# Another DMA queue for one K tile, a key that the rope writes twice, and later transposes in a two-layer trunk on one core

## The chip, the cores and the metric

One Trainium2 chip, one core. The metric is the device time of one execution in microseconds. The kernel before takes 310.66 us, the median of three runs (310.49 to 310.70). All intermediate times are microseconds from the start of the profiled span, unless marked otherwise.

## The reference

Two layers of a post-norm trunk on x of 256 tokens by 1024 features (float32): `x = layer_norm(ALPHA * x + sublayer(x))`. The first is an attention in which an indexer selects 64 keys for each query, the second a stick-breaking attention. The change lies in the first:

```python
q, k, v, g, qi, wi, ki = split(x @ w_in)          # 16 heads of 64, indexer: 8 heads of 64, one key
q = apply_rope(q); k = apply_rope(k)
qi = apply_rope(qi); ki = apply_rope(ki)
rel = relu(einsum('bqhd,bsd->bqhs', qi, ki) * 64 ** -0.5)
score = einsum('bqhs,bqh->bqs', rel, wi * 8 ** -0.5)
score = where(key_chunk <= q_chunk, score, -inf)
_, idx = top_k(score, 64)
p = softmax(logits of q with the selected k)
return (p @ selected v * silu(g)) @ w_out
```

The second layer computes `z = q @ k`, a reversed running sum of `log_sigmoid(-z)` over earlier keys, and weights v with `exp(log_sigmoid(z) + sum)`, with the same gate, projection and norm.

## The kernel before, in words

Products of float32 values are made of three products of a shorter type (fp32r): every operand is split into a high part and a remainder. `split` (lines 65 to 68) does it for weights: ACT casts the high part `wh` (L66), DVE subtracts to get the remainder `wl` (L67). `feat_split` (L250 to L256) does the same for what comes out of a transpose, and `pad_split` (L258) splits a key for two heads in two halves of 64 partitions each, so it issues two ACT casts and two DVE remainders (L252, L253).

**Start.** x, transposed, and the indexer's weights arrive as eight K tiles of `x_idx` (L168 to L176), 420 KB each. Tile 0 comes in three pieces, two on SP's DMA queue and one on ACT's; tiles 1 and 3 are issued from ACT, the others from SP. PE multiplies them tile by tile (L231). Then weights come in chunks of 512 KB from `w_all`, all on SP's queue in program order (`load`, L79). There are four raw buffers, so the load of a chunk waits until DVE has made the remainder of the chunk four before it. I call the chunks w0, w1 and so on.

**Indexer.** `rope` (L214 to L221) makes two products (L218 with the cosine, L219 with the sine) and one sum (L221) on DVE. For each of two token tiles it is called for five heads and for four, the last of which is the indexer's key. POOL copies the key once more behind itself (L241), so that one transpose of two heads gives the key in both halves of the partitions. `select` transposes the doubled key (L275), splits it, transposes the eight query heads in two groups of four (L281), splits them (`qih`, `qil`), and then makes scores: three matmuls for each pair of heads and token tile (`mm3`, L141 to L143), a relu on ACT (`rel`, L294) and two score updates on DVE (L297). The selection of the 64 largest follows on DVE (L304, L305).

**Blocks of q, k and v.** `tok_block` (L121) multiplies four chunks into two of the three PSUM banks of pool `pp` (L118). `q_block` ropes its two banks, transposes them in eight transposes (L329) and splits them (L255, L256), all at its end. `k_block` ropes only, and `keys0` transposes a pair of heads later (L404). `v_block` copies its banks on ACT (L357). Line 527 mixes q, k and v of the first half with `select`; line 528 lists what fills in behind: k, q and v of the second half, the gates (L150, L152), the output projection (L118 with `oh`, `ol`).

**Attention.** The loop at L535 runs a pipeline over head pairs: keys, logits (L141 to L143), a softmax (DVE L423, ACT L428 and L433), transposes of it (PE L442 to L444, ACT copy L446), value matmuls (L372, L373).

The text above gives an order of program; a scheduler then fixes the order of instructions on each engine, and each engine runs its own in that order and waits where an operand is not there.

Of the kernel before, what the change touches and what calls it, by code (L numbers as in the profile page):

```python
# [14 lines left out]
P = 128  # L15
# [27 lines left out]
def trunk(ctx: ExitStack, tc: tile.TileContext, x_rows, x_idx, w_all, consts, lnp, out):  # L43
# [60 lines left out]
    def bank(p, w=512):  # L104
        return p.tile([P, 512], F32, name="bank", tag="bank")[:, :w]
# [6 lines left out]
    def tok_part(outs, src, wc, c):  # L112

        for xp, wp in ((0, 0), (1, 0), (0, 1)):
            for t, ps in outs:
                for k in range(2):
                    kk = 2 * c + k
                    nc.tensor.matmul(ps, src[kk][xp][:, t * P:(t + 1) * P], wc[wp][:, k, :],  # L118
                                     start=kk == 0 and xp + wp == 0, stop=kk == 7 and wp == 1)

    def tok_block(src):  # L121

        ps = [bank(pp) for _ in range(NT)]
        for c, wc in enumerate(load_block()):
            if c:
                yield
            tok_part(list(enumerate(ps)), src, wc, c)
        return ps

    def mix(*gens):  # L130
# [37 lines left out]
    for k in range(KT):  # L168
        raw = wraw.tile([P, CW], F32, name="raw", tag="raw")[:, :S + IDX_W]
        if k:  # L170
            (nc.scalar.dma_start if k in (1, 3) else load)(raw, x_idx[k])
        else:
            first = S + IDX_A
            load(raw[:, :S], x_idx[k, :, :S])
            nc.scalar.dma_start(raw[:, S:first], x_idx[k, :, S:first])
            load(raw[:, first:], x_idx[k, :, first:])  # L176
        wh = wspl.tile([P, CW], F32R, name="wh", tag="wh")[:, :IDX_W]
        wl = wspl.tile([P, CW], F32R, name="wl", tag="wl")[:, :IDX_W]
        if k:
            split(xTh[:, k], xTl[:, k], raw[:, :S])  # L180
        else:
            nc.vector.tensor_copy(xTh[:, k], raw[:, :S])
            nc.vector.tensor_sub(xTl[:, k], raw[:, :S], as32(xTh[:, k]))
        for c in cuts if k == 0 else (slice(0, IDX_W),):
            copy = split(wh[:, c], wl[:, c], raw[:, S + c.start:S + c.stop])
            if k == 0:
                tc.keep_in_program_order(copy)
        idx_w.append((wh, wl))
# [22 lines left out]
        nc.gpsimd.memset(as32(zl), 0.0)  # L211
        zpad.append((zh, zl))

    def rope(dst, ps, heads, t):  # L214
        v = ps.rearrange("p (h d) -> p h d", d=HD)
        a = wk.tile([P, 8, HD], F32, name="ra", tag="ra")[:, :heads]
        b = wk.tile([P, 8, HD], F32, name="rb", tag="rb")[:, :heads]
        nc.vector.tensor_mul(a, v, cos[:, t, None, :].to_broadcast([P, heads, HD]))  # L218
        nc.vector.tensor_mul(b, v, sin[:, t, None, :].to_broadcast([P, heads, HD]))  # L219
        halves = [u.rearrange("p h (e d) -> p h e d", e=2) for u in (dst, a, b)]  # L220
        nc.vector.tensor_add(halves[0], halves[1], halves[2][:, :, ::-1, :])  # L221


    psi = [[bank(at) for _ in range(2)] for t in range(NT)]
# [12 lines left out]
    for t in range(NT):  # L237
        r = sb.tile([P, D], F32, name=f"ri{t}", tag=f"x{t}")[:, :10 * HD].rearrange("p (h d) -> p h d", d=HD)
        rope(r[:, :5], psi[t][0][:, :IDX_A], 5, t)
        rope(r[:, 5:9], psi[t][1][:, :4 * HD], 4, t)  # L240
        nc.gpsimd.tensor_copy(r[:, 9], r[:, 8])  # L241
        w = few.tile([P, IH], F32, name=f"wi{t}")
        nc.vector.tensor_scalar(w, psi[t][1][:, 4 * HD:4 * HD + IH], float(np.float32(IH ** -0.5)), None,
                                op0=OP.mult)
        ri.append(r)
        wi.append(w)
# [22 lines left out]
    def select():  # L269

        for _ in range(2):
            yield
        pt = bank(at)
        for t in range(NT):
            nc.tensor.transpose(pt[:, t * P:(t + 1) * P], ri[t][:, 8:10, :], ident)  # L275
        pad_split(kz, pt[:, :S])
        for j in range(2):
            pt = bank(at)
            for a in range(2):
                for t in range(NT):  # L280
                    nc.tensor.transpose(pt[:, (2 * a + t) * P:(2 * a + t + 1) * P],  # L281
                                        ri[t][:, 4 * j + 2 * a:4 * j + 2 * a + 2, :], ident)
            pv = pt.rearrange("p (a s) -> p a s", a=2)
            feat_split(qih[:, 2 * j:2 * j + 2], qil[:, 2 * j:2 * j + 2], pv)
        yield
        scores = [sb.tile([P, (t + 1) * P], F32, name=f"sc{t}") for t in range(NT)]
        for j in range(4):
            for t in range(NT):
                n = (t + 1) * P
                ts = slice(t * P, (t + 1) * P)  # L290
                pv = bank(at, 2 * n).rearrange("p (a s) -> p a s", a=2)
                mm3(pv, qih[:, j, ts], qil[:, j, ts], kz[0][:, :, :n], kz[1][:, :, :n], True, True)
                rel = wk.tile([P, 2, S], F32, name="rel", tag="p256")[:, :, :n]
                nc.scalar.activation(rel, pv, AF.Relu, scale=SCALE)  # L294
                for a in range(2):
                    h = 2 * j + a
                    nc.vector.scalar_tensor_tensor(scores[t], rel[:, a, :], wi[t][:, h:h + 1],  # L297
                                                   scores[t] if h else adm[t], op0=OP.mult, op1=OP.add)
            yield
        for t in range(NT):  # L300
            sc = scores[t]
            for i in range(TOPK // 8):
                m8 = sml.tile([P, 8], F32, name="m8")
                nc.vector.max(out=m8, in_=sc)  # L304
                nc.vector.match_replace(out=sc, in_to_replace=m8, in_values=sc, imm_value=NEG_REP)  # L305
                if i % 2:
                    yield
            nm = sb.tile([P, (t + 1) * P], F32, name=f"nm{t}")
            nc.vector.tensor_scalar(nm, sc, 0.9 * NEG_REP, -NEG_BIG, op0=OP.is_gt, op1=OP.mult)
            negm.append(nm)  # L310
# [7 lines left out]
    def q_block(half):  # L318
        ps = yield from tok_block(xs)
        rr = []  # L320
        for t in range(NT):
            r = wk.tile([P, 8, HD], F32, name=f"rq{t}", tag=f"s{t}")
            rope(r, ps[t], 8, t)
            rr.append(r)
        for j in range(2):
            pt = bank(at)
            for a in range(2):
                for t in range(NT):
                    nc.tensor.transpose(pt[:, (2 * a + t) * P:(2 * a + t + 1) * P],  # L329
                                        rr[t][:, 4 * j + 2 * a:4 * j + 2 * a + 2, :], ident)  # L330
            for a in range(2):
                g = 4 * half + 2 * j + a
                feat_split(qh[g], ql[g], pt[:, a * S:(a + 1) * S], -SCALE)
        yield

    def k_block(half):
# [379 lines left out]
```

## Time and profile before

| what | us |
|---|---|
| median of three runs | 310.66 (310.49 to 310.70) |
| the profiled execution | 310.33 |
| its span | 308.4 |
| PE busy | 296.5 (96%) |
| DVE busy | 245.1 (79%) |
| ACT busy | 203.7 (66%) |
| POOL busy | 9.0 (3%) |

The profile is of one execution, whose time is 1.9 us more than its span. A busy share is a mean over stages; by stretch, another engine can be the one without a gap. The mean granted clock of TensorE is 0.995 of full speed.

### The profile page before, as it was taken

Reading aid. Unit: us, or ns where it says so; the run is one execution under the profiler, and the core shown is the slowest. Engines: PE = TensorE matmul, PEld = TensorE weight load, DVE = VectorE, ACT = ScalarE, POOL = GpSimd, SP = SyncE. Lnnn points to the kernel's source line nnn. Section 1 sums busy time; section 2 is a strip of 40 time slices with the busy share of each in tenths; the row PEclk is TensorE's granted clock in tenths of the full one; section 3 lists DMA queues with packets and bytes.
Section 4 is the critical chain, followed back from the end, with each engine's and each line's share of the span. In section 5 each row is a group of like instructions: output and inputs, shape, how many; then the busy total and the mean of one; then the engine's idle time right before and its main releaser. Section 6 shows DMA issues by size and latency. Waiting matters only on the chain.

```text
span 308.4 us, 4668 instructions
## 1 busy us (share of the span) xinstructions
PE 296.5 (96%) x1640; PEld 248.7 (81%) x1640; DVE 245.1 (79%) x517; ACT 203.7 (66%) x427; POOL 9.0 (3%) x18
## 2 busy tenths in 40 slices
PE   7998999999999999999999999999999999999990
PEld 4886888787888888878788888888888888877790
DVE  3669999899999687977499573886898999884385
ACT  4656673475569999998415374767599999985200
POOL 3011000000000000000010100000000000000011
PEclk9999999999999999999999999999999999999997
DMA  7796543876068854254424459785543353000003
GB/s 262 229 349 189 177 156 112 275 258 218 9 240 270 307 191 140 105 216 134 166 68 132 142 154 385 251 292 167 190 132 88 118 160 115 0 2 1 0 16 122
DMA packets 14567, 50.40 MB, mean 163 GB/s; under 512 B 1616, under 2 KB 2000, under 8 KB 14544
## 3 DMA queue, kind: packets, MB, share of 16 engines
q1 hardware_dynamic: 14112, 49.08, 48.5%
q10 hardware_dynamic: 432, 1.02, 0.9%
q8 instruction: 13, 0.21, 0.3%
q14 instruction: 10, 0.08, 0.1%
HBM read 49.05 MB, written 1.05 MB: 162 GB/s over the span
## 4 chain that ended last, share of the span: by engine, by line
PE 83%; DVE 7%; DMA 5%; ACT 1%; issue 1%; POOL 0%; DVEq 0%; SPq 0%; ACTq 0%
PE bank L118 36%; PE bank L150 19%; PE bank L152 10%; PE bank L372 3%; DVE wl L67 3%; DMA raw<-x_idx 3%; DMA raw<-w_all 2%; PE bank L141 1%; PE bank L373 1%; PE bank L605 1%; PE bank L142 1%; PE bank L143 1%; ACT wh L66 1%; DVE sc L305 1%; PE bank L584 1%
## 5 line engine op out<-in xcount | busy, mean ns | idle before, releaser
L66 ACT ACTIVATE wh<-raw 128x1024 fp32r<-128x1024 f32 (+2 forms) x89 | 90.0, 1017 | 52.0 <-DMA raw<-w_all 30.8
L67 DVE TENSOR_TENSOR wl<-raw,wh 128x1024 fp32r<-128x1024 f32 (+2 forms) x89 | 103.5, 1166 | 25.3 <-ACT wh L66 24.9
L118 PE MATMUL bank<-wh,xT 128*128 128x512 f32 x192 | 49.8, 395 | 1.4 <-ACT vt L357 0.7
L150 PE MATMUL bank<-yT,wh 128*128 128x512 f32 x192 | 48.6, 395 | 0.0
L118 PEld LDWEIGHTS bank<-wh,xT 128*128 128x128 f32 x192 | 35.3, 188 | 9.4 <-ACT vt L357 1.2
L150 PEld LDWEIGHTS bank<-yT,wh 128*128 128x128 f32 x192 | 34.5, 188 | 7.1 <-issue 0.3
L152 PEld LDWEIGHTS bank<-yT,wl 128*128 128x128 f32 x192 | 26.2, 190 | 1.9
L152 PE MATMUL bank<-yT,wl 128*128 128x256 f32 x192 | 26.7, 282 | 0.0
L118 PE MATMUL bank<-wl,xT 128*128 128x512 f32 x96 | 26.7, 390 | 0.0
L118 PEld LDWEIGHTS bank<-wl,xT 128*128 128x128 f32 x96 | 18.0, 188 | 3.9
L118 PE MATMUL bank<-wh,oh 128*128 128x512 f32 (+1 forms) x80 | 20.8, 355 | 0.0
L118 PE MATMUL bank<-wh,ol 128*128 128x512 f32 (+1 forms) x80 | 20.7, 350 | 0.0
L118 PE MATMUL bank<-wl,oh 128*128 128x512 f32 (+1 forms) x80 | 20.3, 349 | 0.0
L118 PE MATMUL bank<-wh,yT 128*128 128x512 f32 x64 | 17.4, 391 | 0.0
L150 PE MATMUL bank<-xT,wh 128*128 128x512 f32 x64 | 16.3, 396 | 0.0
L118 PEld LDWEIGHTS bank<-wh,ol 128*128 128x128 f32 x80 | 14.0, 189 | 2.1 <-issue 0.2
L118 PEld LDWEIGHTS bank<-wl,oh 128*128 128x128 f32 x80 | 14.0, 189 | 2.0 <-issue 0.2
L118 PEld LDWEIGHTS bank<-wh,oh 128*128 128x128 f32 x80 | 13.5, 189 | 2.3 <-issue 0.6
L428 ACT ACTIVATE p<-ml,mx 128x128 f32<-128x128 f32 (+1 forms) x32 | 14.2, 448 | 1.2 <-DVE mx L423 1.1
L155 DVE TENSOR_TENSOR bank<-bank,low 128x256 f32<-128x256 f32 x32 | 13.6, 424 | 0.7 <-ACT low L154 0.4
L118 PEld LDWEIGHTS bank<-wh,yT 128*128 128x128 f32 x64 | 11.9, 188 | 2.4
L150 PEld LDWEIGHTS bank<-xT,wh 128*128 128x128 f32 x64 | 11.7, 188 | 2.3
(138 smaller groups left out, 508.1 us busy)
## 6 DMA issues: line engine op xcount, KB each, us to landing
raw<-w_all SPq DMA_DIRECT2D x80, 512.0 KB, 4.2
raw<-x_idx SPq DMA_DIRECT2D x5, 420.0 KB, 4.2
gb<-lnp SPq DMA_DIRECT2D x4, 512.0 KB, 6.2
x<-x_rows SPq DMA_DIRECT2D x2, 512.0 KB, 4.4
y<-x SPq DMA_DIRECT2D x4, 256.0 KB, 2.0
raw<-x_idx ACTq DMA_DIRECT2D x2, 420.0 KB, 5.2
cs<-consts SPq DMA_DIRECT2D x1, 512.0 KB, 6.8
raw<-x_idx ACTq DMA_DIRECT2D x1, 160.0 KB, 2.7
```

The lines of the kernel that those rows point to most:

```text
L66: copy = nc.scalar.activation(h, src, AF.Copy)
L67: nc.vector.tensor_sub(lo, src, as32(h))
L118: nc.tensor.matmul(ps, src[kk][xp][:, t * P:(t + 1) * P], wc[wp][:, k, :], start=kk == 0 and xp + wp == 0, stop=kk == 7 and wp == 1)
L141: nc.tensor.matmul(ps, sh, mh, start=first, stop=False)
L142: nc.tensor.matmul(ps, sh, ml, start=False, stop=False)
L143: nc.tensor.matmul(ps, sl, mh, start=False, stop=last)
L150: nc.tensor.matmul(ps, wh[:, k, :], both[:, k], start=k == 0, stop=k == 7)
L152: nc.tensor.matmul(ps[:, :S], wl[:, k, :], high[:, k], start=False, stop=k == 7, skip_group_check=True)
L155: nc.vector.tensor_add(ps[:, :S], ps[:, :S], low)
L305: nc.vector.match_replace(out=sc, in_to_replace=m8, in_values=sc, imm_value=NEG_REP)
L372: nc.tensor.matmul(po[rs, n * S:(n + 1) * S], vt[0][:, hs], p0(i), start=True, stop=False)
L428: nc.scalar.activation(p[:, i, :], m[:, i, :], AF.Exp, bias=mx[:, c], scale=-1.0, accum_out=sm[:, c])
```

## The change

Four things change. Of the K tiles, only tile 2 is issued from ACT; tiles 1 and 3 go to SP's queue. The rope of the last four heads of the indexer writes three heads with one sum and the key twice with a second one, and POOL's copy is gone. The indexer's queries are transposed and split first, the key last. The transposes of a q block are put into a list and issued behind the second chunk of the next block.

```diff
+    late = []
+
     def tok_block(src):
...
             tok_part(list(enumerate(ps)), src, wc, c)
+            if c == 1:
+                while late:
+                    late.pop(0)()
         return ps
...
         if k:
-            (nc.scalar.dma_start if k in (1, 3) else load)(raw, x_idx[k])
+            (nc.scalar.dma_start if k == 2 else load)(raw, x_idx[k])
...
-    def rope(dst, ps, heads, t):
+    def rope(dst, ps, heads, t, twice=False):
...
-        nc.vector.tensor_add(halves[0], halves[1], halves[2][:, :, ::-1, :])
+        one = heads - twice
+        nc.vector.tensor_add(halves[0][:, :one], halves[1][:, :one], halves[2][:, :one, ::-1, :])
+        if twice:
+            last = [u[:, one:].to_broadcast([P, 2, 2, HD // 2]) for u in (halves[1], halves[2][:, :, ::-1, :])]
+            nc.vector.tensor_add(halves[0][:, one:], *last)
...
         rope(r[:, :5], psi[t][0][:, :IDX_A], 5, t)
-        rope(r[:, 5:9], psi[t][1][:, :4 * HD], 4, t)
-        nc.gpsimd.tensor_copy(r[:, 9], r[:, 8])
+        rope(r[:, 5:10], psi[t][1][:, :4 * HD], 4, t, twice=True)
...
-        pt = bank(at)
-        for t in range(NT):
-            nc.tensor.transpose(pt[:, t * P:(t + 1) * P], ri[t][:, 8:10, :], ident)
-        pad_split(kz, pt[:, :S])
         for j in range(2):
...
             feat_split(qih[:, 2 * j:2 * j + 2], qil[:, 2 * j:2 * j + 2], pv)
+        pt = bank(at)
+        for t in range(NT):
+            nc.tensor.transpose(pt[:, t * P:(t + 1) * P], ri[t][:, 8:10, :], ident)
+        pad_split(kz, pt[:, :S])
         yield
...
-        for j in range(2):
-            pt = bank(at)
-            for a in range(2):
-                for t in range(NT):
-                    nc.tensor.transpose(pt[:, (2 * a + t) * P:(2 * a + t + 1) * P],
-                                        rr[t][:, 4 * j + 2 * a:4 * j + 2 * a + 2, :], ident)
-            for a in range(2):
-                g = 4 * half + 2 * j + a
-                feat_split(qh[g], ql[g], pt[:, a * S:(a + 1) * S], -SCALE)
+
+        def turn_q():
+            for j in range(2):
+                pt = bank(at)
+                for a in range(2):
+                    for t in range(NT):
+                        nc.tensor.transpose(pt[:, (2 * a + t) * P:(2 * a + t + 1) * P],
+                                            rr[t][:, 4 * j + 2 * a:4 * j + 2 * a + 2, :], ident)
+                for a in range(2):
+                    g = 4 * half + 2 * j + a
+                    feat_split(qh[g], ql[g], pt[:, a * S:(a + 1) * S], -SCALE)
+
+        late.append(turn_q)
         yield
```

In the changed kernel, the rope is at L225 to L232, the query and key transposes of the indexer at L287 and L293, the three score matmuls at L147 to L149, and the transposes of a q block at L341.

On ACT, behind the cast of chunk w6, stand the splits of the indexer's key (`zh_177`) and queries (`qih`). Before:

```order
L66 ACTIVATE wh<-raw 128x1024 x7
L252 ACTIVATE zh_177<-bank 64x256
L252 ACTIVATE qih<-bank 128x512 x2
L252 ACTIVATE zh_177<-bank 64x256
L66 ACTIVATE wh<-raw 128x1024 x3
L294 ACTIVATE rel<-bank 128x2x128
L294 ACTIVATE rel<-bank 128x512
```

After:

```order
L66 ACTIVATE wh<-raw 128x1024 x7
L262 ACTIVATE qih<-bank 128x512 x2
L262 ACTIVATE zh_177<-bank 64x256
L66 ACTIVATE wh<-raw 128x1024
L262 ACTIVATE zh_177<-bank 64x256
L66 ACTIVATE wh<-raw 128x1024
L304 ACTIVATE rel<-bank 128x2x128
L66 ACTIVATE wh<-raw 128x1024
L304 ACTIVATE rel<-bank 128x512
```

The query casts moved ahead of both halves of the key, a weight cast stands between the halves, and the first two relus stand behind one more weight cast each.

On PE, the rows behind chunk w3 (its x8 and x4) lead to the first score matmuls. Before:

```order
L118 MATMUL bank<-wh,xT 128x512 x4
L118 MATMUL bank<-wl,xT 128x512 x2
L118 MATMUL bank<-wh,xT 128x512 x7
L118 MATMUL bank<-wl,xT 128x512 x2
L329 MATMUL bank<-cs,rq_439 128x128 x2
L141 MATMUL bank<-zh_177,qih 128x256
L142 MATMUL bank<-zl_178,qih 128x256
L143 MATMUL bank<-zh_177,qil 128x256
```

After:

```order
L118 MATMUL bank<-wh,xT 128x512 x4
L118 MATMUL bank<-wl,xT 128x512 x2
L147 MATMUL bank<-zh_177,qih 128x256
L147 MATMUL bank<-zh_177,qih 128x512
L147 MATMUL bank<-zh_177,qih 128x256
L147 MATMUL bank<-zh_177,qih 128x512
L118 MATMUL bank<-wh,xT 128x512
L148 MATMUL bank<-zl_178,qih 128x256
L149 MATMUL bank<-zh_177,qil 128x256
```

The first score matmuls, which read both halves of the key, moved ahead of nine matmuls of chunks w4 and w5, and the transposes of the first q block (L329) are no longer there.

On ACT again, between the softmax of the second and third head pair (`p_993` before, `p_1103` for the third), the casts around a key (`zh_181`). Before:

```order
L433 ACTIVATE p_1006<-p_1006,rc 128x256 x2
L252 ACTIVATE zh_181<-bank 64x256
L66 ACTIVATE wh<-raw 128x1024 x2
L252 ACTIVATE zh_181<-bank 64x256
L428 ACTIVATE p_1103,sm<-ml_1102,mx 128x128 x2
L428 ACTIVATE p_1116,sm<-ml_1115,mx 128x256 x2
```

After:

```order
L262 ACTIVATE zh_181<-bank 64x256
L447 ACTIVATE p_988<-p_988,rc 128x256 x2
L262 ACTIVATE zh_181<-bank 64x256
L265 ACTIVATE qh_331<-bank 128x256
L265 ACTIVATE qh_333<-bank 128x256
L66 ACTIVATE wh<-raw 128x1024
L265 ACTIVATE qh_332<-bank 128x256
L265 ACTIVATE qh_334<-bank 128x256
L66 ACTIVATE wh<-raw 128x1024
L442 ACTIVATE p_1103,sm<-ml_1102,mx 128x128 x2
```

Both halves of the key are ahead of the two weight casts now, and the casts of the second half's queries (`qh_331` to `qh_334`) came in between them.

## Rows read from the trace of the kernel before

**Rows 1.** The page, busy time, share of the span and instructions:

```profile
PE 296.5 (96%) x1640; PEld 248.7 (81%) x1640; DVE 245.1 (79%) x517; ACT 203.7 (66%) x427; POOL 9.0 (3%) x18
```

**Rows 2.** Busy time by stretch: stretch, length, then each engine's busy us (instructions):

```profile
35.00:48.00 13.00, 13.00 (x68) 11.00 (x67) 12.84 (x27) 8.82 (x17) 0.00 (x0) 1.00 0.44 129
...
101.00:133.00 32.00, 32.00 (x207) 27.94 (x206) 25.94 (x74) 31.83 (x85) 0.00 (x0) 1.00 0.57 192
```

**Rows 3.** PE's waits up to 78 us: line, releaser, us in total, times, longest:

```profile
PE bank L275 <- POOL ri L241: 1.1, 1, 1.1
PE bank L118 <- DVE rb L219: 0.7, 1, 0.7
```

**Rows 4.** PE's timeline, start: start, us, line, tiles, count [idle time before, releaser]:

```profile
6.63 1.26 PE L231 MATMUL bank<-wh,xT 128*128 128x320 f32 x8
...
9.03 1.35 PE L231 MATMUL bank<-wh,xT 128*128 128x320 f32 x8 [0.60 <-ACT wh L66]
...
19.02 2.12 PE L118 MATMUL bank<-wh,xT 128*128 128x512 f32 x8
...
27.33 0.27 PE L275 MATMUL bank<-cs,ri 128*128 128x128 f32 x1
28.70 0.33 PE L275 MATMUL bank<-cs,ri 128*128 128x128 f32 x1 [1.09 <-POOL ri L241]
...
29.65 2.10 PE L118 MATMUL bank<-wh,xT 128*128 128x512 f32 x8
...
32.51 1.07 PE L118 MATMUL bank<-wh,xT 128*128 128x512 f32 x4
```

**Rows 5.** POOL's timeline, the second copy of the key:

```profile
27.47 1.17 POOL L241 COPY ri<-ri 128x64 f32<-128x64 f32 x1 [2.08 <-DVE ri L221]
```

**Rows 6.** DMA issues from 1.1 to 1.4 and 1.5 to 1.8 us: KB, us to landing:

```profile
raw<-x_idx ACTq DMA_DIRECT2D x1, 420.0 KB, 3.9
...
raw<-x_idx SPq DMA_DIRECT2D x1, 132.0 KB, 3.5
...
raw<-x_idx SPq DMA_DIRECT2D x1, 420.0 KB, 6.3
```

**Rows 7.** ACT's timeline, casts of w0, w7, w8 and w15:

```profile
17.91 1.06 ACT L66 ACTIVATE wh<-raw 128x1024 fp32r<-128x1024 f32 x1 [1.84 <-DMA raw<-w_all]
...
32.08 1.06 ACT L66 ACTIVATE wh<-raw 128x1024 fp32r<-128x1024 f32 x1 [0.48 <-DMA raw<-w_all]
34.66 1.06 ACT L66 ACTIVATE wh<-raw 128x1024 fp32r<-128x1024 f32 x1 [1.51 <-DMA raw<-w_all]
...
59.64 1.06 ACT L66 ACTIVATE wh<-raw 128x1024 fp32r<-128x1024 f32 x1 [1.56 <-PE bank L118]
```

**Rows 8.** DVE's timeline, sums and products of ropes:

```profile
24.66 0.42 DVE L221 TENSOR_TENSOR ri<-ra,rb 128x256 f32<-128x256 f32 x1
25.00 0.48 DVE L218 TENSOR_TENSOR ra<-bank,cs 128x320 f32<-128x320 f32 x1
...
48.26 0.69 DVE L218 TENSOR_TENSOR ra<-bank,cs 128x512 f32<-128x512 f32 x1 [0.30 <-PE bank L118]
```

**Rows 9.** PE's timeline later: after the v wait, and two blocks of value matmuls:

```profile
61.24 1.45 PE L118 MATMUL bank<-wh,xT 128*128 128x512 f32 x5 [0.72 <-ACT vt L357]
...
103.58 0.66 PE L372 MATMUL bank<-pT,vt 128*64 128x256 f32 x4
...
105.08 0.39 PE L141 MATMUL bank<-zh,qh 128*128 128x256 f32 x1
...
133.79 1.31 PE L118 MATMUL bank<-wh,oh 128*128 128x512 f32 x4
...
136.85 0.66 PE L372 MATMUL bank<-pT,vt 128*64 128x256 f32 x4
...
139.08 0.38 PE L141 MATMUL bank<-zh,qh 128*128 128x256 f32 x1
```

**Rows 10.** ACT's timeline, a weight cast ahead of the exponentials:

```profile
97.42 1.06 ACT L66 ACTIVATE wh<-raw 128x1024 fp32r<-128x1024 f32 x1 [0.56 <-DMA raw<-w_all]
```

## The prediction

> **What bounds the kernel now.** I began with the busy times of the engines: PE is busy for 96% of the span [rows 1]. So I asked the busy times by stretch: from 35 to 48 us PE has 13.00 of 13.00 us and DVE 12.84, and from 101 to 133 PE has 32.00 and ACT 31.83 [rows 2]. In the first of them DVE sets the pace together with PE, in the second ACT does. The list of PE's waits says where PE stood still: 1.1 us for POOL's copy of the indexer's key, 0.7 for a rope product, and 0.72 for the copies of v [rows 3, 9]. Last I read the timelines of PE, ACT and DVE around the lines that the diff touches. One idle time is in no list: a block of sixteen value matmuls takes 1.50 us at 103.58 (to the next row's 105.08), but 2.23 at 136.85 (to 139.08) [rows 9]. Those 0.73 us, and 0.24 more in four matmuls at 133.79 that take 1.31 where 1.07 is usual [rows 4, 9], are time in which PE follows an ACT that has no gap [rows 2]. I call it the **late stall**, 0.97 us.
>
> Shifts below are against the profiled execution (310.33 us, of which 308.4 are span); the median of the runs is 0.33 longer, and I add the same shift to it. A difference of 0.2%, 0.62 us, is about what a measurement of this kernel can tell from none.
>
> **K tiles: 0.** Tile 1 now waits on SP's queue behind both pieces of tile 0, tile 2 goes on ACT's. In the trace ACT's second transfer, issued at about 1.2, took 3.9 us and landed at 5.1; SP's third, issued at about 1.6, took 6.3 and landed at 7.9 [rows 6]. I place tile 2 at 5.1 now, and tile 1, which has little beside it from 5 on, at 6.3 (bounds 5.1 and 7.9, the two rows). From landing to PE's first use takes 1.1 (7.9 to 9.03 [rows 4]), so PE, which started k=1 at 6.63 without a wait [rows 4], starts it at 7.4 and loses 0.8, and k=2 follows without its 0.60 us of idle time [rows 4], 9.03 as before. An earlier PE would gain nothing either: chunk w0 starts at 19.02, just behind its cast, which ran from 17.91 to 18.97 [rows 4, 7], and that cast waits for its DMA. With tile 1 at 7.9, PE is 1.64 late (one K tile's pitch); that is rival D.
>
> **The key's second copy: -1.27, then +1.0.** The second transpose of the key started at 28.70, 1.37 after the first, where 0.1 is usual [rows 4], since POOL's copy started at 27.47, after DVE's sum, and took 1.17 [rows 5]. That goes. The query transposes come first and need heads 0 to 7 alone, and the doubled key is ready by the time its own two run, so PE begins chunk w3 at 28.4 instead of 29.65. It pays later. On ACT the two large casts of the index queries now precede the key's first half, and a weight cast (w7) stands between the halves. That cast began at 32.08 when its data came [rows 7], lasts 1.06, and the second half follows at 33.2, done at 33.56. PE gets to its first score matmuls at 32.51 - 1.27 + 1.36 = 32.6 (one half of chunk w4, six matmuls of 0.23) [rows 4] and waits there for 1.0 us. Bounds: 0.6, if w7's data come 0.4 earlier, since a DVE remainder releases their load, and 1.27, where nothing of the gain is left. PE keeps about 0.3 of the gain.
>
> **DVE between 27 and 48 us: +0.2.** The sum over four heads took 0.42 and the next operation began 0.34 after it; one over five heads took 0.48 [rows 8]. So a head costs 0.06, a sum over three 0.28 and one over the two copies 0.22 until the next can begin: +0.16 for each of two tiles, +0.32. I take off 0.15 (0 to 0.4) for an earlier w0, because K tile 3 now has SP's queue behind tile 1 and frees its buffer a little sooner. The order adds three waits: the first score's relu stands on ACT behind w8's cast (34.66 + 1.06 [rows 7]), +0.39; the second behind w9's, +0.30; the last query split behind w10's, +0.25. Gone are the 0.30 in front of the k rope [rows 8], 0.29 between the first four score updates and 0.20 between the halves of the key, which no longer alternate with the queries. Sum: 0.32 - 0.15 + 0.94 - 0.79 = +0.32; walking the stream operation by operation gives 48.47 instead of 48.26, so I take +0.2 (-0.4 to +0.5).
>
> **Query transposes: 0.** Eight transposes and four evictions move behind the next block's second chunk. The cover is PE's own work. But the casts of the v banks, which PE awaits at 61.24 [rows 9], stand on ACT behind a weight cast at 59.64 [rows 7] whose load DVE's remainder four chunks earlier releases. So PE's lead is spent in that wait, which grows from 0.72 to about 1.2, and PE leaves at 61.24 + 0.2. The wait of 0.7 for the rope of the second k half [rows 3] goes the same way: DVE's order puts the two sine products ahead of a weight remainder now, and PE meets the wait earlier, so PE is at +0.2 again at 77 us and, with no idle time found up to 101, there too.
>
> **The late stall: -0.95.** Moving the second half's queries also clears ACT at 95 to 100. Before, two weight casts stood between the halves of a key, and the second waited 0.56 for its data [rows 10], with the key's half and eight exponentials behind it. Now both halves are ahead of those casts and the query casts are elsewhere. ACT's gain is between 0 and that cast with its wait, 1.62; I take the middle, 0.8, since the work only moves and some of it comes back before 107. From there the orders are alike and ACT has no gap, so ACT is 0.8 earlier at 137. PE, at +0.2, drops as much of the late stall as ACT allows: 0.2 - 0.97 = -0.77, and ACT allows -0.8. I book -0.95 (0 to -0.97).
>
> Sum: 0 - 1.27 + 1.0 + 0.27 (the lead spent, DVE) + 0.2 - 0.95 = **-0.75**, 309.58 for the profiled execution and **309.9** against the median.
>
> **The rivals.** **A, the forecast**, 309.4 to 310.4, chance 0.40. For it: ACT's share from 101 on. Against it: nothing in the profile names the late stall, I infer it from a pace.
>
> **B, no change**: DVE and ACT set every later landmark, ACT's gain is used up before 107, and the +0.2 stays: 310.3 to 311.0, centre 310.86, chance 0.26. For it: 12.84 of 13.00 us of DVE and 31.83 of 32.00 of ACT. By the Trainium skill ("Perfetto Trace Analysis", Optimization Strategy), the engine to relieve is the most contended one of each regime. By that rule the change, which relieves POOL and gives DVE 0.32 us more, can only end at 310.9; the trace agrees for 35 to 48 us, and not after 77, where PE has no listed idle time.
>
> **C, the whole gain**: the key's split is not late for the scores, PE's 1.27 stays, the waits for v and for that rope (0.7 each) shrink with DVE, and the late stall goes as well. The gain is 1.3 to 2.0: 308.7 to 309.4, chance 0.14. Against it: both waits hang on DVE, which gets more to do.
>
> **D, slower**: tile 1 on SP's queue decides. If it lands past 6.4, each further microsecond moves PE through k=1 to w0, whose cast no longer covers it, and the index rope with it. At 7.9 PE is 1.64 late at 19, DVE's rope nearly as much, and the removed POOL wait is no longer reached; with 0.3 kept that is +1.3 and 311.9; down to 311.3 for 7.3. Chance 0.20. For it: SP's third transfer took 6.3. Against it: that one shared the lanes with ACT's third. The Trainium skill ("DMA: Bandwidth & Descriptors", Issuing engines are not separate DMA queues) says that all queues interleave on the same 16 engines and another issuer only saves issue time. By that rule D cannot happen, the order of issue decides and tile 1 lands near 5; the rows agree in part, for SP's piece of 132 KB and ACT's 420 KB, issued together, took 3.5 and 3.9 us: the share of a transfer is not its size alone.
>
> **The numbers.** Faster by over 0.2% (under 310.04): eight tenths of A and all of C, 0.46. Slower (over 311.28): D, 0.20. The rest, 0.34, is B and the slow part of A. The range leaves out the lower half of C and the upper half of D, some 0.17: 308.9 to 311.4. A alone would have 309.4 to 310.4.
>
> **What would show it.** Right: k=1 starts near 7.4 and k=2 near 9.03; ten transposes without a gap near 27.4; a wait of about 1 us for ACT's second half of the key near 32.6; the k rope on DVE at 48.5; a wait of 1.2 for the v copies; the block at 136.85 in 1.6 us or less. Wrong: PE starts w0 later than 19.3 (D); the v wait shrinks (C); the late stall is still there (B).

## The result and the profile after

The change makes the kernel slower: 312.03 us (median of 13 runs, 310.61 to 313.68) against 310.49 for the kernel before on the same chip (13 runs, 309.08 to 311.49). The ratio is 1.0056 [1.0039, 1.0072], so about 1.7 us are lost. The forecast was 309.9 in a range of 308.9 to 311.4: the sign was wrong, and the time lies outside the range.

| what | before | after |
|---|---|---|
| the profiled execution | 310.33 | 312.03 |
| its span | 308.4 | 310.1 |
| DVE's remainder of w3 starts | 27.33 | 28.15 |
| DVE's first rope product of k (the "k rope") | 48.26 | 49.72 |
| PE's first output projection | 133.79 | 135.07 |
| PE's third block of value matmuls | 136.85 | 138.65 |

The first part of the page of the kernel after, and the engines of the chain that ended last (the profile follows it back from the last instruction, at each step to what released it):

```profile
PE 298.1 (96%) x1640; PEld 250.5 (81%) x1640; DVE 245.7 (79%) x519; ACT 202.7 (65%) x427; POOL 7.6 (2%) x16
...
PE 66%; ACT 14%; DVE 12%; DMA 6%; issue 1%; DVEq 0%; SPq 0%; ACTq 0%
```

No busy time differs from [rows 1] by more than 1.8 us. The chain runs over PE for 66% of the span, where it was 83% before, and over ACT for 14%, where it was 1%: other engines hold PE up more often. PE's waits after (line, releaser: us in total, times, longest) show what took POOL's place:

```profile
PE bank L242 <- ACT wh L66: 1.1, 2, 0.6
PE bank L118 <- DVE rb L226: 1.0, 2, 0.8
PE bank L118 <- ACT vt L371: 0.8, 1, 0.8
PE bank L118 <- DVE sg L410: 0.4, 1, 0.4
PE bank L147 <- issue: 0.3, 1, 0.3
```

POOL's 1.1 us [rows 3] are gone. The wait for the K tiles' casts and the one for v are 0.2 and 0.1 longer, the rope's is 0.3 longer, and a new one, for the gate `sg`, stands in the output projection. PE's timeline after (start, us, instruction, count, idle time before it):

```profile
8.48 1.95 PE L242 MATMUL bank<-wh,xT 128*128 128x320 f32 x8
...
10.80 1.25 PE L242 MATMUL bank<-wh,xT 128*128 128x320 f32 x8
...
20.62 2.00 PE L118 MATMUL bank<-wh,xT 128*128 128x512 f32 x8
...
28.81 1.03 PE L287 MATMUL bank<-cs,ri 128*128 128x128 f32 x8
29.68 0.38 PE L293 MATMUL bank<-cs,ri 128*128 128x128 f32 x2
29.82 2.09 PE L118 MATMUL bank<-wh,xT 128*128 128x512 f32 x8
...
34.47 0.94 PE L147 MATMUL bank<-zh,qih 128*128 128x256 f32 x4 [0.30 <-issue]
...
62.66 1.20 PE L118 MATMUL bank<-wh,xT 128*128 128x512 f32 x4 [0.78 <-ACT vt L371]
...
135.07 0.71 PE L118 MATMUL bank<-wh,oh 128*128 128x512 f32 x2
136.14 0.72 PE L118 MATMUL bank<-wh,oh 128*128 128x512 f32 x2 [0.35 <-DVE sg L410]
...
138.65 0.66 PE L386 MATMUL bank<-pT,vt 128*64 128x256 f32 x4
...
140.84 0.39 PE L147 MATMUL bank<-zh,qh 128*128 128x256 f32 x1
```

Beside [rows 4]: K tile 1 is computed at 8.48 instead of 6.63 and chunk w0 at 20.62 instead of 19.02. The ten transposes now stand without a gap. Beside [rows 9]: PE leaves the v wait at 62.66, 1.42 later. The late stall is still there: the sixteen value matmuls take 2.19 us (138.65 to 140.84; before 2.23), and the output projection ahead of them takes 3.58 instead of 3.06 (135.07 to 138.65).

DVE's timeline after, from the index rope to the k rope, and in the third head pair:

```profile
20.43 0.49 DVE L225 TENSOR_TENSOR ra<-bank,cs 128x320 f32<-128x320 f32 x1 [0.73 <-PE bank L242]
...
28.15 3.49 DVE L67 TENSOR_TENSOR wl<-raw,wh 128x1024 fp32r<-128x1024 f32 x3
...
37.31 0.35 DVE L307 SCALAR_TENSOR_TENSOR sc<-rel,wi,cs 128x128 f32<-128x128 f32 x1 [0.44 <-ACT rel L304]
...
38.75 0.48 DVE L307 SCALAR_TENSOR_TENSOR sc<-rel,wi,cs 128x256 f32<-128x256 f32 x1 [0.22 <-ACT rel L304]
...
45.54 0.42 DVE L266 SCALAR_TENSOR_TENSOR ql<-bank,qh 128x256 fp32r<-128x256 f32 x1 [0.19 <-ACT qh L265]
...
49.72 0.68 DVE L225 TENSOR_TENSOR ra<-bank,cs 128x512 f32<-128x512 f32 x1
...
90.93 2.34 DVE L67 TENSOR_TENSOR wl<-raw,wh 128x1024 fp32r<-128x1024 f32 x2
```

From w3's remainder to the k rope DVE takes 21.57 us (28.15 to 49.72), before 20.93 (27.33 to 48.26): the three waits of 0.44, 0.22 and 0.19 are in it. The last row is the remainders of w22 and w23, back to back; before they stood apart:

```profile
84.38 1.23 DVE L67 TENSOR_TENSOR wl<-raw,wh 128x1024 fp32r<-128x1024 f32 x1
...
88.71 1.22 DVE L67 TENSOR_TENSOR wl<-raw,wh 128x1024 fp32r<-128x1024 f32 x1
```

What hangs on them shows on ACT, whose timeline after has the casts of w7, w26 and w27, and the row `th` from which DVE makes the half of the gate `sg` that the first output projection waits for:

```profile
32.91 1.06 ACT L66 ACTIVATE wh<-raw 128x1024 fp32r<-128x1024 f32 x1 [1.26 <-DVE qil L263]
33.99 0.38 ACT L262 ACTIVATE zh<-bank 64x256 fp32r<-64x256 f32 x1
...
95.60 1.06 ACT L66 ACTIVATE wh<-raw 128x1024 fp32r<-128x1024 f32 x1 [0.17 <-DMA raw<-w_all]
...
98.74 1.06 ACT L66 ACTIVATE wh<-raw 128x1024 fp32r<-128x1024 f32 x1 [1.53 <-DMA raw<-w_all]
...
135.19 0.38 ACT L404 ACTIVATE th<-bank 128x256 f32<-128x256 f32 x1
```

Before, w26 was cast at 89.32 and w27 at 95.79, and the same `th` was

```profile
133.43 0.38 ACT L390 ACTIVATE th<-bank 128x256 f32<-128x256 f32 x1
```

So at the projection ACT is 1.76 later than before and PE 1.28 (135.07 against 133.79). Busy times by stretch (columns as in [rows 2]), first three of after:

```profile
35.00:48.00 13.00, 13.00 (x68) 11.02 (x67) 12.13 (x24) 8.23 (x15) 0.00 (x0) 1.00 0.44 137
77.00:101.00 24.00, 24.00 (x119) 20.10 (x118) 22.12 (x64) 16.43 (x46) 0.00 (x0) 1.00 0.50 173
101.00:133.00 32.00, 32.00 (x208) 27.90 (x207) 26.77 (x68) 31.70 (x86) 0.00 (x0) 1.00 0.58 194
```

and then the second of them in the kernel before:

```profile
77.00:101.00 24.00, 24.00 (x123) 20.06 (x122) 23.12 (x65) 17.55 (x48) 0.00 (x0) 1.00 0.53 180
```

PE looks the same in both, 24.00 of 24.00. But ACT does 1.1 us less from 77 to 101, and behind that it has no gap (31.70 of 32.00) in which to catch up. A part of the 1.1 is only that the whole kernel is later by then, PE by 1.28; what ACT lost beyond that is the 0.48 by which it is later than PE. The chain of the kernel after, traced from 77 to 150 us, shows the way from the load of w27 to PE (start, us, what):

```profile
93.34 5.38 DMA raw<-w_all
98.74 1.06 ACT wh L66
99.80 1.26 ACT p L442 x6
...
135.20 0.43 DVE zl L263
135.66 0.43 DVE sg L410
136.14 2.58 PE bank L118 x10
```

The load starts where w23's remainder ended (90.93 + 2.34). Between its cast and 135 the chain is ACT but for some 2 us of DVE at 108 to 110. In the kernel before, the same stretch of the chain is PE alone.

### The profile page after: what moved, and what is told of

It reads as the page before. It is cut to its first block, busy times and chain, and to the rows that moved or that the text cites. A ratio compares the mean times of both kernels' runs of the same rounds, so it can differ in the third digit from the quotient of the medians.

```text
span 310.1 us, 4672 instructions
## 1 busy us (share of the span) xinstructions
PE 298.1 (96%) x1640; PEld 250.5 (81%) x1640; DVE 245.7 (79%) x519; ACT 202.7 (65%) x427; POOL 7.6 (2%) x16
## 4 chain that ended last, share of the span: by engine, by line
PE 66%; ACT 14%; DVE 12%; DMA 6%; issue 1%; DVEq 0%; SPq 0%; ACTq 0%
PE bank L118 27%; PE bank L156 14%; PE bank L158 7%; PE bank L242 5%; DMA raw<-w_all 5%; ACT wh L66 4%; DVE wl L67 3%; ACT p L442 3%; PE bank L386 2%; ACT p L447 2%; DVE sc L315 2%; DMA raw<-x_idx 1%; PE bank L619 1%; ACT pT L460 1%; DVE m L314 1%
## 5 line engine op out<-in xcount | busy, mean ns | idle before, releaser
L67 DVE TENSOR_TENSOR wl<-raw,wh 128x1024 fp32r<-128x1024 f32 (+2 forms) x89 | 103.2, 1165 | 25.1 <-ACT wh L66 24.8
```

The lines of the kernel that those rows point to most:

```text
L67: nc.vector.tensor_sub(lo, src, as32(h))
```

## The experiments

All ratios are to the kernel before on the same chip. Two stretches tell the kernels apart: **A**, on DVE, from the remainder of w3 to the k rope, and **B**, on PE, from the first output projection to the fourth block of value matmuls; the late stall lies in B. Both are read from one profiled execution each. The last columns set A + B, against the mean of the two profiles of the kernel before (34.21), beside the measured difference, which is the ratio's distance from 1 times 310.2 us.

| kernel | A | B | A + B against before | measured us, interval |
|---|---|---|---|---|
| before | 20.93 | 13.44 | | |
| before, again (e4) | 20.90 | 13.15 | | |
| K tiles alone (e1) | 20.93 | 13.66 | +0.4 | +0.2 [-0.5, +0.9] |
| first q block late alone (e5) | 20.90 | 13.21 | -0.1 | +0.4 [-0.2, +1.1] |
| second q block late alone (e6) | 21.05 | 12.49 | -0.7 | -0.5 [-1.1, +0.2] |
| key last alone (e7) | 20.89 | 13.21 | -0.1 | -0.2 [-0.7, +0.4] |
| rope twice alone (e8) | 20.46 | 12.92 | -0.8 | -0.2 [-0.8, +0.5] |
| rope twice, more warming (e11) | 20.48 | 12.88 | -0.9 | -0.8 [-1.5, -0.2] |
| second q block late, more warming (e12) | 20.93 | 12.49 | -0.8 | -0.9 [-1.6, -0.3] |
| rope twice, second q block late (e9) | 20.49 | 13.96 | +0.2 | +0.3 [-0.4, +1.0] |
| rope twice, key last (f3) | 21.36 | 12.93 | +0.1 | -0.3 [-0.7, +0.1] |
| rope twice, first q block late (f4) | 20.95 | 12.88 | -0.4 | one run |
| the change without its K tiles (e2) | 21.31 | 13.99 | +1.1 | +1.1 [+0.4, +1.8] |
| the change, second q block in place (e10) | 21.31 | 12.85 | -0.1 | -0.2 [-0.9, +0.6] |
| the change, more warming (e3) | 20.92 | 13.93 | +0.6 | +0.8 [+0.3, +1.4] |
| the change | 21.57 | 13.93 | +1.3 | +1.7 [+1.2, +2.2] |

The stretches were chosen after the runs, as those that moved. Except for e8 (0.6), their sum comes within 0.5 us of the measured difference. For f1 and f2 below, which are not in the table, it does not (+0.2 and +0.5 against -2.4 and -1.8), as their gain lies outside A and B. The start of A itself varies from 26.4 to 28.2 in these profiles, in no order that the edits explain: it is 26.41 in e8 and 27.80 in e9, whose engines have the same order up to there.

**First set: which half of the change.** e1 has the K tiles alone. e2 has everything else. e3 is the whole change with `WARM`, the number of the matmuls of 512 columns ahead of K tile 0 (L169), raised. e4 is the kernel before once more.

```diff
-            (nc.scalar.dma_start if k in (1, 3) else load)(raw, x_idx[k])
+            (nc.scalar.dma_start if k == 2 else load)(raw, x_idx[k])
```

> The kernel before with the change of the K tiles' queues alone; every engine's order of compute is the one of before. Theory 1 (the loss is made in the first 11 us: the pieces of tile 0 and tile 1 come later, PE stands still at 4 to 6 us and runs its index matmuls at half pace until about 10 us): chunk w0 starts near 20.6 instead of 19.0, and the time is 1.0 to 1.6 us over the kernel before. Theory 2 (the loss is made by the new order on ACT and DVE between 28 and 140 us, the first 11 us are made up at POOL's wait and later): within 0.4 us of the kernel before.

310.27, ratio 1.0006 [0.9984, 1.0029]. w0 started at 19.88, 0.86 late, and the k rope at 48.17, where it was before: the delay is absorbed between them. The queue alone costs nothing that can be measured. Its B, 13.66, is the longest with before's order of DVE and ACT.

e2 is the change with that one line as it was before.

> The changed kernel with the K tiles on the queues of the kernel before (1 and 3 from ACT). Theory 1: chunk w0 starts near 19.0, k=2 near 9.0, and the time is 0.2 to 1.0 us under the kernel before, as forecast for the rest of the change. Theory 2: 1.0 to 1.5 us over the kernel before, with the wait on the v copies still ending near 62.5 and the late block of value matmuls still 2.2 us.

311.55, ratio 1.0035 [1.0012, 1.0058]. w0 started at 18.61, early, and yet the loss is there: A is 0.4 longer, B 0.7 longer than the mean of before. So most of the loss has nothing to do with the K tiles. What they add on top, 1.0056 against 1.0035, is inside the intervals.

```diff
-WARM = 6
+WARM = 9
```

> The changed kernel with nine matmuls on zeros at the start instead of six, so that PE is busy until about 5.4 us. If idle time at 4 to 6 us is what keeps the index matmuls at half pace: their pitch (264 columns) falls from 0.22 to 0.11 us by 7 us, k=2 starts near 9.2 instead of 10.8, and the time is 0.8 to 1.5 us under the changed kernel. If the late data alone set the loss: k=2 at 10.8 or later and no gain.

310.89, ratio 1.0027 [1.0011, 1.0044]. K tile 2 was computed at 8.94 instead of 10.80 and w0 at 18.78; the loss halves but stays, and B is 13.93, as in the change.

> The kernel before, unchanged, for a second profile of it: how far the landings of tile 0 (3.2, 3.5, 4.7 us), the start of k=2 (9.03) and that of w0 (19.02) move between two executions. Theory 1 needs them within 0.4 us.

310.38 in its one run. A is 0.03 from the first profile, B 0.29. With e1, B spreads over 0.51 (13.15 to 13.66) in one order of DVE and ACT, so a single profile's shift of B by less than that means little; 13.93 to 13.99, in all four kernels that have both the rope's edit and the late second q block, lies outside it.

**Second set: each of the other parts alone.** In each kernel one part stands in the code of before. For the q blocks:

```diff
-        late.append(turn_q)
+        turn_q() if half else late.append(turn_q)
```

(e5: the first block's transposes late, the second's in place) and the reverse, `late.append(turn_q) if half else turn_q()` (e6).

> The kernel before, with the transposes of the first q block alone put behind the next block's second chunk; the order of ACT changes in two places (26 to 38 of its rows) and nowhere later. Theory 2a (the loss comes from the few rows around the scores, 28 to 48 us, where DVE waits for relus behind weight casts): 0.3 to 0.8 us over the kernel before, the k rope on DVE at 48.6 or later instead of 48.2. Theory 2b (it comes from the order of ACT after 75 us, which moved with the edit of the rope): within 0.3 us of the kernel before.

310.27, ratio 1.0013 [0.9992, 1.0034]: nothing measurable.

> The kernel before, with the transposes of the second q block alone put behind the v block's second chunk; nothing changes before 80 us. Theory 2a: within 0.3 us of the kernel before. Theory 2b, if the moved query casts are what leaves ACT idle before 101 us and full after: 0.4 to 1.0 us over, and the stretch from the first output projection matmul to the third block of value matmuls, 3.0 to 3.3 us in the kernel before, takes 3.6. If the rope's edit is what moves ACT's order: no change, and that stretch stays under 3.3.

309.65, ratio 0.9985 [0.9963, 1.0008]. Here the late stall is gone, as its PE timeline shows:

```profile
133.68 1.18 PE L118 MATMUL bank<-wh,oh 128*128 128x512 f32 x4
...
136.62 0.66 PE L387 MATMUL bank<-pT,vt 128*64 128x256 f32 x4
...
138.12 0.39 PE L147 MATMUL bank<-zh,qh 128*128 128x256 f32 x1
```

The sixteen value matmuls take 1.50 us (136.62 to 138.12), and B is 12.49, 0.95 under the first profile of before and 0.66 under the second.

e7 has the key last and POOL's copy as before; e8 has the rope's second key and the key first.

```diff
-        rope(r[:, 5:9], psi[t][1][:, :4 * HD], 4, t)
-        nc.gpsimd.tensor_copy(r[:, 9], r[:, 8])
+        rope(r[:, 5:10], psi[t][1][:, :4 * HD], 4, t, twice=True)
```

> The kernel before, POOL's copy kept, with the indexer's queries transposed and split first and the key last; the order changes in a few rows around 30 us alone. My prediction's step (the query casts ahead of the key hide POOL's copy, the key's second half comes late for the scores) gives 0 to -0.3 us. Theory 2a: 0 to +0.5 with a later k rope on DVE. Theory 2b: within 0.3 us.

310.12, ratio 0.9994 [0.9976, 1.0013]. With the queries' eight transposes ahead of the key, PE's wait for POOL falls from 1.1 to 0.3, and the wait for v grows from 0.7 to 1.3: a wait that went came back 30 us later.

> The kernel before, with the rope writing the key twice in place of POOL's copy, and nothing else; but the scheduler then orders ACT from its 51st to its 112th row in another way (75 to 140 us). POOL's wait of 1.1 us goes, DVE gets 0.3 us more. Theory 2b: 0.4 to 1.2 us over the kernel before, with more idle time on ACT between 77 and 101 us (6.4 us before, 7.9 in the changed kernel's variant) and the stretch from the first output projection matmul to the third block of value matmuls at 3.6 us. Theory 2a: at most +0.3.

310.03, ratio 0.9994 [0.9973, 1.0015]. A is 0.47 shorter, not longer, though DVE has two more instructions. The scheduler put both halves of the program after this edit into another order, so the cost of the extra sum can't be read from it.

Each part alone is free or a little better, and together they are 1.7 us worse. So neither the few rows around the scores (theory 2a) nor one part's new order on ACT (theory 2b) is enough. Something must come from parts together.

**Third set: pairs.** DVE's order of instructions is fixed when the kernel is built. Count the rows of the trace ahead of the remainder of w22 that are not remainders of L67: 124 in before, e5, e6 and e7; 132 in e8; 142 in e2, e3 and the change. The edits of the rope and of the second q block together move it past ten more operations: eight rows of softmax maxima, a rope sum and a reciprocal. That remainder frees a raw buffer, so it releases the load of w26. e9 has these two edits alone; e10 is the change with the second q block in place, which brings the count back to 132.

> The kernel before with two parts of the change: the rope writes the key twice, and the second q block's transposes go behind the v block's second chunk. Each alone cost nothing. Together the scheduler puts DVE's remainder of chunk w22 ten DVE operations later than with the rope's edit alone. Theory 3 (this late remainder holds a raw buffer, so w26 and w27 load and cast late, ACT stands idle before 99 us and enters its stretch without gaps with more left to do): the cast of w27 starts 3 us or more after that of w26, the stretch from the first output projection matmul to the third block of value matmuls takes 3.6 us (2.9 to 3.3 in kernels of before's order), and the time is 0.3 to 1.5 us over the kernel before. Rival (the loss needs the key's place or the first q block's): within 0.3 us of the kernel before, stretch under 3.2.

310.68, ratio 1.0009 [0.9986, 1.0033]. B is 13.96 and the wait for `sg` is there (0.38), as in the change, where each of the two edits alone had shortened B to 12.92 and 12.49. w27's cast came 3.14 behind w26's (97.15 and 94.01), to the hundredth as in the change (98.74 and 95.60). ACT's `th` came at 133.61 and PE's projection at 133.46: against before, ACT is later than PE by 0.51, and B is longer by 0.52. The whole kernel is not clearly slower than before, since its A is 0.44 shorter.

> The changed kernel with one thing undone: the second q block's transposes stay at its end. PE, DVE and ACT keep the changed kernel's order but for some rows around 80 to 97 us, among them DVE's remainder of w22, which goes ten operations earlier. Theory 3: the time falls by 0.8 to 1.8 us against the changed kernel, to the kernel before's or up to 0.6 under it, and the stretch takes 2.9 to 3.1 us. Rival (K tiles, key last and the first q block carry the loss): at most 0.3 under the changed kernel.

310.15, ratio 0.9995 [0.9971, 1.0019]: the loss is gone. DVE's timeline of this kernel has the remainders of w22 and w23 apart:

```profile
89.01 1.21 DVE L67 TENSOR_TENSOR wl<-raw,wh 128x1024 fp32r<-128x1024 f32 x1
...
92.13 1.21 DVE L67 TENSOR_TENSOR wl<-raw,wh 128x1024 fp32r<-128x1024 f32 x1
```

The load of a weight chunk issued from 92.6 to 94 us (KB, us to landing) shows what this does. First the change:

```profile
raw<-w_all SPq DMA_DIRECT2D x1, 512.0 KB, 5.4
```

and e10:

```profile
raw<-w_all SPq DMA_DIRECT2D x1, 512.0 KB, 3.5
```

The load is w27's, issued at the same time in both (93.34 in the change, 93.39 in e10). In the change it runs beside that of w26, which w22's remainder released only at 92.20 (in e10 at 90.29), and takes 1.9 longer. The other kernels with four buffers say the same: where the two were issued 1.1 apart (the change, e2, e3, e9), w27's took 5.4 to 5.9, and where they were 3.1 apart or more (the other twelve), 3.5 to 3.7. ACT's timeline of e10 has the casts of w26 and w27:

```profile
95.17 1.07 ACT L66 ACTIVATE wh<-raw 128x1024 fp32r<-128x1024 f32 x1
...
97.46 1.06 ACT L66 ACTIVATE wh<-raw 128x1024 fp32r<-128x1024 f32 x1
```

w27 is cast at 97.46 and not at 98.74, ACT does 17.48 us of work from 77 to 101, and B is 1.08 shorter than in the change. PE reached the first output projection at 135.01, as late as in the change (135.07), but ACT's `th` came at 134.06, 1.13 earlier, and PE made up 0.6 of its 1.2 us within B. The chain from 77 to 150 us is PE alone again, as in twelve others of the eighteen profiles; it leaves PE in the change, e2, e3, e9, and in e1, whose B is the longest of the rest. No run moves the remainder of w22 alone: between e9 and e8, or the change and e10, 18 rows of DVE and 17 of ACT differ. That the remainder and not ACT's own new order makes w27 late is read from the issue and landing of the loads.

e11 is e8, and e12 is e6, with `WARM` 9.

> A version that may beat both kernels: the kernel before with the rope writing the key twice and nine matmuls on zeros at the start. The rope's edit alone gave -0.3 us (-0.8 to +0.5), the longer start took 1.1 us off the changed kernel. If the two add: 0.5 to 1.2 us under the kernel before. If the start is covered by DVE's stream, which reached the k rope at 48.2 to 48.3 us for starts of w0 between 19.0 and 19.9: no more than the rope's edit alone.

309.38, ratio 0.9973 [0.9953, 0.9994].

> The other version that may beat both: the kernel before with the second q block's transposes late and nine matmuls on zeros at the start. The first part alone gave -0.5 us (-1.1 to +0.2). If the longer start adds to it: 0.7 to 1.3 us under the kernel before; if it is covered: 0.3 to 0.7 under.

309.36, ratio 0.9970 [0.9950, 0.9989]. Either part alone, with nine warming matmuls, is faster than before by some 0.3%. No run has the nine with the rest as before, so how much of this is the warming's own stays open; without it the two measured 0.9994 and 0.9985, inside each other's intervals. B (12.88 and 12.49) is as without the warming.

**Fourth set: the ring of raw buffers, and A.** If the loss in B comes through raw buffers freed too late, more of them must remove it. f1 is the change and f2 is before, each with

```diff
-    wraw = pool("wraw", 4)
-    wspl = pool("wspl", 8)
+    wraw = pool("wraw", 6)
+    wspl = pool("wspl", 7)
```

> The changed kernel with six raw buffers and seven pairs of split buffers instead of four and eight; the scheduler moves further rows. If the ring of four raw buffers is how late remainders make late casts: ACT's waits on weight loads (31 us in sum) fall by half or more, ACT is ahead at 99 us, the stretch from the first output projection matmul to the third block of value matmuls is under 3.1 us, and the time falls to 1 to 3 us under the changed kernel. If the casts are late for their place in ACT's order alone: waits fall, but the stretch stays at 3.5 us and the time within 0.5 us of the changed kernel.

307.51, ratio 0.9922 [0.9909, 0.9935].

> The kernel before with the same six and seven buffers. By the ring theory ACT's waits on weight loads fall by half or more here too, PE's waits for the v copies (0.7 us) go, and the time is 0.5 to 1.5 us under the kernel before; if DVE's stream alone sets the pace up to 77 us, the waits fall and the time stays within 0.4 us.

308.15, ratio 0.9942 [0.9930, 0.9955]. Both beat both kernels, and with six buffers the change is not the slower one. B is 12.49 in both; the remainder of w3 starts at 25.90 and 23.89, A takes 21.94 and 22.23, and from B's end to the span's it is 1.2 and 0.8 less than in before. ACT's stretch of f1 now has slack:

```profile
101.00:133.00 32.00, 32.00 (x207) 27.91 (x206) 26.16 (x78) 30.51 (x87) 0.00 (x0) 1.00 0.51 164
```

30.51 where 31.70 stood: w27 was cast at 88.26, ten us earlier than in the change. The pools set the scheduler's order too (w22's remainder stands behind 118 such rows in f1), so this shows that the ring matters, not how much of it is depth and how much order. f3 is e8 with the key last, f4 is e8 with the first q block late, to find what lengthens A.

> The rope writes the key twice and the key is transposed and split last; the first q block in place, the second too. If the key's place lengthens DVE's stretch from the remainder of w3 to the k rope: 21.1 to 21.5 us; if it is the late transposes of the first q block: 20.4 to 20.6, as with the rope's edit alone.

309.93, ratio 0.9990 [0.9977, 1.0002]; A is 21.36, 0.90 longer than in e8.

> The rope writes the key twice and the first q block's transposes go behind the next block's second chunk; the key first. If the late transposes lengthen DVE's stretch from the remainder of w3 to the k rope: 21.1 to 21.5 us; if it is the key's place: 20.4 to 20.6.

309.21 in its one run; A is 20.95, 0.49 longer than in e8, which is neither of the two forecasts. Beside the rope written twice, both the key's late split and the first q block lengthen A in these profiles. Which does more is not shown: four kernels with the change's order on DVE up to the k rope have an A from 20.92 (e3) to 21.57 (the change). With POOL's copy in place (e7) the same move of the key cost nothing (20.89).

## Why the prediction was wrong

**The late stall, -0.95: the step that failed.** It measured +0.49 in B (13.44 to 13.93). The mechanism exists: e6, which has the move of the second half's queries alone, shortens B by 0.66 to 0.95. But the step took ACT's order as the whole story ("both halves are ahead of those casts") and put ACT 0.8 earlier at 137; it came 1.76 later (`th` at 135.19, before 133.43). The casts wait for data, the data for a raw buffer, and that for a remainder in DVE's order, which I read only up to 48 us and around 77. In the change the remainders of w22 and w23 came late and together, w27's cast and the exponentials behind it waited 1.53 for data just ahead of ACT's gapless stretch, and the stall grew by the 0.48 that ACT was later than PE. Nor were the query casts "elsewhere": they run from 94.77 to 97.2, in the stretch that the step took for cleared (before from 91.25 to 93.4), as the order after, shown with the change, has them. e9 shows B growing for the pair alone, e10 that taking one of the pair away undoes it, and in f1, with more buffers, it is gone. From -0.95 to +0.49 are 1.4 us, the larger part of the whole error of 2.5 (-0.75 forecast, +1.7 measured).

**DVE between 27 and 48 us, +0.2: mis-sized.** The k rope came at 49.72, 1.46 late, and not at 48.47. 0.64 of that is A, where I had +0.94 of new waits, -0.79 of old ones and +0.32 of sums; new waits of 0.85 are there. The 0.64 is not the order's alone: with nine warming matmuls the same order has an A of 20.92 (e3). The other 0.82 is A's late start, and I had taken 0.15 off there. Which of it belongs to the change stays open: DVE stood 0.73 idle for PE at 20.43, but the starts of A differ as much between kernels with the same order up to there (26.41 in e8, 27.80 in e9).

**K tiles, 0: right in time, wrong in place.** k=1 started at 8.48 and k=2 at 10.80, not at 7.4 and 9.03, w0 at 20.62, later than the 19.3 that I named as the sign of rival D. Tile 1 landed at 6.67, near the 6.3 that I had placed it at, and PE was at work on tile 0 until 8.48, at half its later pace (last section). In the order of before, e1 shows no cost that can be measured. The Trainium skill ("DMA: Bandwidth & Descriptors", Issuing engines are not separate DMA queues) says that another issuer only saves issue time. The time of e1 agrees. The landing near 5 that I drew from it did not come: the 420 KB of tile 1, issued between 1.4 and 1.75 on SP's queue, took 5.0 and so came past 6.4, where the same tile, issued at about 1.2, came at 5.1 from ACT's [rows 6].

**The key: right in the main.** The transposes are gapless and the wait for POOL is gone. The second half of the key was cast at 33.99, not 33.2, because w7's cast came at 32.91, not 32.08 [rows 7]: 0.83 late, as DVE's remainder of w3, which frees its raw buffer, was 0.82 late. (The row names DVE's `qil`, which ended at 32.84; w7's load, issued at 29.40, landed at 32.82.) PE's wait in front of the scores is small in the change (0.3), as PE was itself late, and 1.5 and 1.3 in e2 and e3, where it was early.

**The v wait and the query transposes: right in kind.** The lead is spent at v, whose copies came late as DVE did (62.66 against 61.44 forecast). e5 and e6 show no cost of the moved transposes by themselves.

**The rivals.** D named almost the measured time (311.9) but not the cause: e1 has its mechanism and no loss. B had the engines right and no loss: DVE and ACT set the landmarks, and they moved. The Trainium skill ("Perfetto Trace Analysis", Optimization Strategy) says that the most-contended engine can change from one regime of a kernel to the next; the trace agrees, with DVE busy for 12.84 of 13.00 us from 35 to 48 and ACT for 31.83 of 32.00 from 101 to 133 [rows 2]. No rival had what happened, an interaction of two edits through a third engine's order. Each chance was given to a single edit's effect, and the range was too narrow on the slow side by 0.6.

## What to carry to other kernels

Judge a combined edit by the whole order that it produces, on all engines, and above all by the instructions that free a ring's buffers: here two edits that were each free or better alone together pushed one remainder past ten more operations, and a stretch that each had shortened by 0.4 and 0.8 us grew by 0.7. An engine without a gap for 30 us can't win back what it idled ahead of that stretch, however idle it looks there. And where casts wait for data again and again, first try a deeper ring: with six raw buffers the kernel before came 0.6% and the change 0.8% under the kernel before, though the order moved with the buffers there.

## What the runs showed of the hardware

TensorE's pace in the first ten us differed between executions in a way that the edits don't order. e6, with the K tiles on their old queues:

```profile
6.62 1.18 PE L242 MATMUL bank<-wl,xT 128*128 128x320 f32 x4
7.60 2.15 PE L242 MATMUL bank<-wh,xT 128*128 128x320 f32 x8
...
10.41 1.23 PE L242 MATMUL bank<-wh,xT 128*128 128x320 f32 x8
11.48 0.71 PE L242 MATMUL bank<-wl,xT 128*128 128x320 f32 x4
```

Four matmuls of 320 columns take 0.98 us at 6.62, or 0.24 for each, and eight take 1.07 at 10.41, 0.13 for each: 1.3 and 2.4 columns in a nanosecond, so about the lower and the upper of TensorE's two levels, 1.2 and 2.4 GHz. The page's clock row reads 9 (90% or more) from the first slice in all of these kernels. But the trace's first record of the granted clock, of full speed, begins only at 10.28 in e6 (10.06 in the change, 4.69 in before), where the spacing changes, and the page counts what lies ahead of it as full. So there the clock is to be read from the matmuls' spacing. Full pace came at 5.3 to 5.9 in before, e2, e4, e5, e7, e9, e10, f2 and f3, at 7.2 in e8, and at 8.7 to 10.3 in f4, e1, f1, the change and e6. Of the four kernels with the new queues and six warming matmuls three are late and one is not; of the eleven with the old queues three are. The three with nine had it between 6.0 and 6.7. Nor do idle times alone decide: in e4 PE stood idle for 0.67 among the matmuls of K tile 0 and was at full pace at 5.85, in e6 it had no such gap and was at 10.3. What decides was not settled. It mattered little: in e6, w0 was 1.2 late, and DVE's remainder of w3 was not.
